# Modulation weights of the mixer's run as fp16 high and low parts, with the conditioning rows as high and low columns of one operand

## The chip, the core and the metric

One core of a Trainium2 chip runs the whole program. TensorE (PE, with its weight loads shown as PEld) multiplies, VectorE (DVE) and ScalarE (ACT) do elementwise work, GpSimd (POOL) does small elementwise work and some DMA issues, SyncE (SP) issues most DMAs in order. The metric is the device time of one execution in microseconds (us); lower is better.

## What is computed

One layer of a hybrid encoder for 512 tokens of a new stream and 8 x 16 tokens of running streams (640 columns, 9 conditioning rows). What matters here:

```python
mod = (jax.nn.silu(c) @ lp['w_ada'] + lp['b_ada'])[:, None, :]
sh_m, sc_m, gt_m, sh_f, sc_f, gt_f = jnp.split(mod, 6, axis=-1)
h = rms_norm(x, lp['g_pre_mix']) * (1 + sc_m) + sh_m
proj = h @ lp['w_in']
...   # attention heads and RWKV-7 heads on proj, both into mix
x = x + gt_m * rms_norm(mix, lp['g_post_mix'])
h = rms_norm(x, lp['g_pre_ffn']) * (1 + sc_f) + sh_f
f, conv_last = conv_ffn(h, conv_prev, lp['w_up'], lp['w_conv_ffn'], lp['w_down'])
x = x + gt_f * rms_norm(f, lp['g_post_ffn'])
```

`w_ada` is 2048 x 12288 in fp32. Its first two of six column blocks (`sh_m`, `sc_m`) are needed before the input projection and are computed in the opening stage; the other four (`gt_m`, `sh_f`, `sc_f`, `gt_f`) are not needed before the output projection has been summed. The change is in these four.

## The kernel before

Large products run on TensorE in fp16 with three passes: a weight tile `[128, 1024]` of fp32 lands in a staging buffer `ws`, ACT writes its high part in fp16 and DVE (`scalar_tensor_tensor`) the low part, both into a buffer `wh`; the matmuls then are high x high, high x low and low x high (`gstep`). `unit` (L379 to L386) does one such tile: a `ws` buffer (`wtile`, 2 buffers, `WS`), a DMA on SP's queue, a `wh` buffer (4, `WH`), the split.

The mixer's run goes from the end of the opening stage to the output projection. Its cover work is 45 chunks of the input projection, each with two units and 96 matmuls in two halves (384 and 256 columns). Between these matmuls stand small jobs: eight RWKV head pairs one after another, each a chain of PE, DVE and ACT steps over blocks of tokens (`S`, `AR`, `VT`, `GB` are its tiles) with round trips through DRAM; eight attention heads; and the generator `ada` (from L1331), the modulation. It works through the four column blocks and for each through 16 row tiles `k`, which makes 64 steps. A step loads two fp32 tiles `wa` of `[128, 1024]` by SP (buffers of their own: tag `wa`, 2) and multiplies `cta` (the conditioning, 128 x 32 columns per `k`, of which 9 are used) with them: four fp32 matmuls of 512 columns, whose outputs stand in four groups of 32 partitions of one PSUM bank. After each four steps DVE adds the bank into `acc`; after 16, four transposes and a DVE addition with the bias finish the block.

The order on PE is fixed in the code. `Interleave` (L143 on) keeps a planned clock: `mm` and the helpers of ACT, DVE and POOL add planned costs to it, and after each k-tile of a projection `pump` lets the waiting generators go on whose planned time has come, `ada` at the lowest priority. A chunk is emitted only when certain heads are far enough (the `while` loop after `ada`); while it may not be, `S.step` moves the planned clock and only the small jobs are emitted. After the 45 chunks come the first products of the output projection (`early`), and then `S.drain(lambda: not S.tasks)` emits what is left of the small jobs before the output projection goes on. The orders on ACT, DVE, POOL and SP are made by a scheduler; each engine runs its list in that order.

## Time and profile before

| | us |
|---|---|
| median of 3 runs (lowest, highest) | 3185.57 (3177.09, 3187.53) |
| the profiled execution | 3185.55 |
| its span, first to last instruction | 3183.7 |
| mixer's run, from the first `wada2` load to the last input-projection matmul | 164 to 1290 |
| first output-projection products and drain of the small jobs | 1290 to 1373 |
| rest of the output projection, FFN | 1373 to 3184 |

The three runs lie within 0.33%. In a timeline row the numbers are start, duration, engine, line, operation, output and inputs, tile size, shape and count; brackets hold idle time before it and what ended it. An fp32 matmul is recorded as two.

### The profile page before, as it was taken

Reading aid. Unit: us, or ns where it says so; the run is one execution under the profiler, and the core shown is the slowest. Engines: PE = TensorE matmul, PEld = TensorE weight load, DVE = VectorE, ACT = ScalarE, POOL = GpSimd, SP = SyncE. Lnnn points to the kernel's source line nnn. Section 1 sums busy time; section 2 is a strip of 40 time slices with the busy share of each in tenths; the row PEclk is TensorE's granted clock in tenths of the full one; section 3 lists DMA queues with packets and bytes.
Section 4 is the critical chain, followed back from the end, with each engine's and each line's share of the span. In section 5 each row is a group of like instructions: output and inputs, shape, how many; then the busy total and the mean of one; then the engine's idle time right before and its main releaser. Section 6 shows DMA issues by size and latency. Waiting matters only on the chain.

```text
span 3183.7 us, 66675 instructions
## 1 busy us (share of the span) xinstructions
PE 3049.7 (96%) x26714; PEld 2075.9 (65%) x26714; DVE 2277.4 (72%) x4347; ACT 1407.5 (44%) x2744; POOL 809.3 (25%) x1508
## 2 busy tenths in 40 slices
PE   6999999999999999789989999999999999999997
PEld 3566666656656566556766677777777777776766
DVE  5454655665556465436788889898999999999875
ACT  4434333343334343334654555454444454544552
POOL 0003213123122120013405424233142231332134
PEclk9999999999999999889999999999999999999998
DMA  9665444534444443355543443533525335254361
GB/s 378 231 207 171 137 142 140 161 127 147 158 141 141 160 135 121 109 175 182 183 149 109 105 130 96 139 107 98 147 93 132 115 92 157 87 124 125 98 229 67
DMA packets 226582, 457.24 MB, mean 144 GB/s; under 512 B 74272, under 2 KB 118432, under 8 KB 226272
## 3 DMA queue, kind: packets, MB, share of 16 engines
q1 hardware_dynamic: 202640, 414.14, 40.4%
q0 software_dynamic: 18160, 32.83, 5.3%
q10 hardware_dynamic: 5472, 6.02, 0.5%
q8 instruction: 209, 3.42, 0.4%
q14 instruction: 101, 0.83, 0.1%
HBM read 425.86 MB, written 26.72 MB: 142 GB/s over the span
## 4 chain that ended last, share of the span: by engine, by line
PE 65%; DVE 9%; DMA 2%; issue 2%; ACT 2%; POOL 1%; SPq 1%; DVEq 0%; ACTq 0%; POOLq 0%
PE ps L269 64%; DVE wh L307 3%; DMA ws<-in_wupT 1%; DVE ws L292 1%; DVE mo L292 1%; PE ps L279 1%; DVE z L307 1%; ACT wh L284 1%; DMA ws<-in_wdnT 1%; SPq L1408 0%; DVE f L307 0%; DVE mo L307 0%; DVE f L292 0%; DMA ckv<-in_ckT 0%; ACT VT L284 0%
## 5 line engine op out<-in xcount | busy, mean ns | idle before, releaser
L269 PEld LDWEIGHTS <-wh 128*128 128x128 f16 x17160 | 1654.5, 98 | 770.7 <-issue 96.6
L269 PE MATMUL ps<-FB,wh 128*128 128x320 f16 x7464 | 1034.4, 301 | 21.7 <-DVE wh L307 5.5
L307 DVE SCALAR_TENSOR_TENSOR wh<-ws,wh 128x1024 f16<-128x1024 f32 (+1 forms) x823 | 803.5, 985 | 219.0 <-ACT wh L284 211.7
L284 ACT ACTIVATE wh<-ws 128x1024 f16<-128x1024 f32 (+1 forms) x823 | 677.8, 834 | 603.6 <-PE ps L269 408.1
L269 PE MATMUL ps<-hT,wh 128*128 128x256 f16 (+3 forms) x4704 | 714.2, 302 | 6.3 <-ACT hT L284 3.9
L269 PE MATMUL ps<-act,wh 128*128 128x320 f16 (+2 forms) x3456 | 475.1, 299 | 6.6 <-ACT wh L284 3.8
L292 DVE TENSOR_TENSOR ws<-ws,ws 128x1024 f32<-128x1024 f32 (+1 forms) x260 | 268.0, 1031 | 13.6 <-DMA ws<-in_wupT 7.8
L269 PE MATMUL ps<-mt,wh 128*128 128x320 f16 x1536 | 219.5, 306 | 13.9 <-DMA mt<-mxd 7.8
L307 DVE SCALAR_TENSOR_TENSOR f<-ps,f 128x320 f32<-128x320 f32 (+2 forms) x336 | 160.7, 483 | 46.9 <-PE ps L269 43.7
L284 ACT ACTIVATE VT<-ps 32x64 f32<-32x64 f32 (+2 forms) x256 | 65.1, 254 | 249.3 <-DVE VT L311 234.1
L307 DVE SCALAR_TENSOR_TENSOR z<-fe,cwv,z 128x656 f32<-128x656 f32 x176 | 162.7, 925 | 4.8 <-ACT z L284 1.6
L420 POOL DMA_DIRECT2D ws<-in_wdnT x96 | 83.3, 867 | 288.1 <-DVE wh L307 131.6
L1456 POOL TENSOR_TENSOR sq<-sq,sq 128x320 f32<-128x320 f32 (+2 forms) x74 | 104.5, 1415 | 194.7 <-ACT sq L284 168.5
L269 PE MATMUL ps<-VT,GB 16*32 16x16 f32 (+4 forms) x2304 | 142.0, 222 | 10.7 <-DVE VT L311 4.0
L284 ACT ACTIVATE act<-z 128x192 f16<-128x192 f32 (+3 forms) x178 | 66.0, 408 | 149.6 <-POOL z L1903 59.0
L269 PEld LDWEIGHTS ps<-VT,GB 32*32 32x32 f32 (+3 forms) x2304 | 80.0, 112 | 78.7 <-issue 39.9
L311 DVE COPY VT<-ps 32x64 f32<-32x64 f32 (+1 forms) x160 | 37.1, 232 | 127.9 <-PE ps L269 119.1
L1920 POOL MEMSET fe<- 128x2 f32 x88 | 12.1, 139 | 443.9 <-DVE z L307 321.5
L296 POOL TENSOR_TENSOR fs<-TU,AU 40x15 f32<-40x15 f32 (+7 forms) x240 | 71.1, 296 | 166.3 <-DMA AU<-gd 149.5
L269 PE MATMUL ps<-wa,cta 128*32 128x256 f32 (+1 forms) x1024 | 111.5, 518 | 0.2 <-DMA wa<-in_wada 0.2
L307 DVE SCALAR_TENSOR_TENSOR S<-S,dcol,ps 128x64 f32<-128x64 f32 x128 | 35.6, 278 | 95.7 <-PE ps L269 94.8
L292 DVE TENSOR_TENSOR act<-z,act 128x320 f16<-128x320 f32 (+3 forms) x160 | 79.2, 524 | 19.8 <-ACT act L284 19.7
(329 smaller groups left out, 3012.0 us busy)
## 6 DMA issues: line engine op xcount, KB each, us to landing
wa<-in_wada SPq DMA_DIRECT2D x192, 512.0 KB
ws<-in_wupT SPq DMA_DIRECT2D x190, 512.0 KB
ws<-in_winT SPq DMA_DIRECT2D x90, 512.0 KB
ws<-in_wdnT SPq DMA_DIRECT2D x96, 384.0 KB
ws<-in_woutT SPq DMA_DIRECT2D x60, 512.0 KB
ws<-in_wdnT POOLq DMA_DIRECT2D x96, 192.0 KB, 3.9
ckv<-in_ckT SPq DMA_DIRECT2D x64, 256.0 KB
ckv<-in_cvN SPq DMA_DIRECT2D x64, 256.0 KB
```

What stands on the lines that cost most here:

```text
L269: nc.tensor.matmul(out, lhsT, rhs, start=start, stop=stop, skip_group_check=True)
L279: nc.tensor.transpose(out, in_, ident)
L284: nc.scalar.activation(out, in_, func, scale=scale, bias=bias)
L292: nc.vector.tensor_tensor(out, a, b, op)
L296: nc.gpsimd.tensor_tensor(out, a, b, op)
L307: nc.vector.scalar_tensor_tensor(out, a, s, b, op0, op1)
L311: nc.vector.tensor_copy(out, a)
L420: nc.gpsimd.dma_start(out, src, accum_op=ADD)
L1456: nc.gpsimd.tensor_tensor(self.acc, self.acc, sq, ADD)
L1920: nc.gpsimd.memset(e[:, 0:2], 0.0)
```

## The change

The fp32 tile of a modulation step now lands in a `ws` buffer (`wtile`, the pool of the input projection's units) and is split by ACT and DVE into fp16 parts in a `wa` buffer of the same bytes (2 buffers). The conditioning is split once into `ct16`: columns 0 to 8 high, 9 to 17 low, the rest zero. A step is then eight fp16 matmuls (high part, then low part, each into the four groups of partitions), and the end of a block adds two column ranges, with 8 small DVE operations in place of one. The planned cost of an fp16 matmul with an output of at most 32 partitions is divided by four.

```diff
         if rhs.dtype == F16:
-            S.pe(n / 2400 + 0.002)
+            S.pe(n / 2400 / (4 if out.shape[0] <= 32 else 1) + 0.002)
...
+    ct16 = mc.tile([P, KD, 32], F16, name="ct16")
...
+        nc.gpsimd.memset(ct16, 0.0)
...
+        act(ct16[:, :, 0:9], cta[:, :, 0:9], AF.Copy)
+        tt(ct16[:, :, 9:18], cta[:, :, 0:9], ct16[:, :, 0:9], SUB)
...
             for k in range(KD):
-                ws = []
+                sts, ws = [], []
                 for u in range(2):
-                    w = lp.tile([P, 1024], F32, tag="wa", bufs=2, name=nm("wa"))
-                    nc.sync.dma_start(w, wada2[i, k, u])
-                    ws.append(w)
+                    sts.append(wtile())
+                    nc.sync.dma_start(sts[u], wada2[i, k, u])
                 S.wait(6.0)
+                for st in sts:
+                    ws.append(lp.tile([P, 2, 1024], F16, tag="wa", bufs=2, name=nm("wa")))
+                    split(ws[-1], st, 1024)
...
-                for u in range(2):
-                    for g in range(2):
-                        q = 2 * u + g
-                        mm(ab[32 * q:32 * q + 32, :], cta[:, k, :], ws[u][:, g * 512:(g + 1) * 512], k % 4 == 0, k % 4 == 3)
+                for z in range(2):
+                    for q in range(4):
+                        g = q % 2
+                        mm(ab[32 * q:32 * q + 32, :], ct16[:, k, :], ws[q // 2][:, z, g * 512:(g + 1) * 512],
+                           k % 4 == 0 and z == 0, k % 4 == 3 and z == 1)
...
-            tt(out.rearrange("p (g s) i -> p g s i", s=4), src, bb.unsqueeze(3).broadcast_to([P, 4, 4, 9]), ADD)
+            o4 = out.rearrange("p (g s) i -> p g s i", s=4)
+            for s in range(4):
+                stt(o4[:, :, s], src[:, :, s, 0:9], 1.0 / SW, bb[:, :, s:s + 1].broadcast_to([P, 4, 9]), MUL, ADD)
+                stt(o4[:, :, s], src[:, :, s, 9:18], 1.0 / SW, o4[:, :, s], MUL, ADD)
```

Three places of the orders, before and after. First SP's loads early in the mixer's run: `in_winT` feeds the input projection, `in_wada2` the modulation. Before:

```order
L383 DMA ws_501_3752<-in_winT 128x1024
L1339 DMA wa_450_3230<-in_wada2 128x1024
L1339 DMA wa_451_3232<-in_wada2 128x1024
L383 DMA ws_503_3757<-in_winT 128x1024
L927 DMA td1_1475<-TU_407_2944 20x16x16 x4
L932 DMA VT_380_2757<-td1_1475 32x10x64 x2
L1339 DMA wa_464_3372<-in_wada2 128x1024
L1339 DMA wa_465_3374<-in_wada2 128x1024
L383 DMA ws_563_4073<-in_winT 128x1024
L383 DMA ws_565_4078<-in_winT 128x1024
```

and after:

```order
L383 DMA ws_746_5114<-in_winT 128x1024
L383 DMA ws_748_5119<-in_winT 128x1024
L1344 DMA ws_775_5310<-in_wada2 128x1024
L1344 DMA ws_776_5312<-in_wada2 128x1024
L383 DMA ws_790_5440<-in_winT 128x1024
L383 DMA ws_792_5445<-in_winT 128x1024
L1344 DMA ws_809_5605<-in_wada2 128x1024
L1344 DMA ws_810_5607<-in_wada2 128x1024
L383 DMA ws_818_5704<-in_winT 128x1024
L383 DMA ws_820_5709<-in_winT 128x1024
L1344 DMA ws_836_5871<-in_wada2 128x1024
L1344 DMA ws_837_5873<-in_wada2 128x1024
```

Before, the modulation's loads went to `wa` and stood at any place among the others; after, both kinds go to the two `ws` buffers, in turn by pairs.

Second PE, at the end of the first long stretch without projection matmuls (it lies behind the twelfth of the 45 chunks in both orders). `wh` is a unit of the chunk that follows, `ident` marks a transpose. Before:

```order
L269 MATMUL ps_714_4962<-ckv_666_4679,aTs_708_4923 32x128 x4
L269 MATMUL ps_714_4962<-ckv_667_4682,aTs_708_4923 32x128 x4
L269 MATMUL ps_714_4962<-ckv_668_4685,aTs_708_4923 32x128 x4
L269 MATMUL ps_714_4962<-ckv_669_4688,aTs_708_4923 32x128 x4
L269 MATMUL ps_714_4962<-vtk_506_3766,aTs_708_4923 32x128 x4
L269 MATMUL ps_694_4857<-S_711_4948,AR_512_3794 64x64 x2
L269 MATMUL ps_694_4857<-VT_514_3796,GB_513_3795 32x64 x2
L269 LDWEIGHTS wh_731_5039
L269 MATMUL ps_734_5047<-hT_92,wh_731_5039 128x384
```

and after:

```order
L269 MATMUL ps_665_4712<-wa_682_4777,ct16_99 32x512
L269 MATMUL ps_738_5057<-GB_559_4085,VT_560_4086 32x96 x10
L269 MATMUL ps_739_5058<-GB_559_4085,VT_560_4086 32x96 x10
L269 MATMUL ps_740_5083<-S_631_4557,AR_558_4084 64x64 x2
L269 MATMUL ps_740_5083<-VT_560_4086,GB_559_4085 32x64 x2
L279 MATMUL ps_741_5095<-ident_69,osbs_514_3799 128x128 x2
L269 LDWEIGHTS wh_747_5116
L269 MATMUL ps_750_5124<-hT_92,wh_747_5116 128x384
```

The last work ahead of the chunk was attention and one RWKV step; now it is the eight fp16 matmuls of a modulation step, a few RWKV rows and a transpose.

Third PE at the end of the drain, where the output projection (`mt`) goes on. Before:

```order
L269 MATMUL ps_2535_16786<-ckv_2521_16735,aTs_2534_16782 32x128 x4
L269 MATMUL ps_2535_16786<-ckv_2522_16738,aTs_2534_16782 32x128 x4
L269 MATMUL ps_2535_16786<-ckv_2523_16741,aTs_2534_16782 32x128 x4
L269 MATMUL ps_2535_16786<-ckv_2524_16744,aTs_2534_16782 32x128 x4
L269 MATMUL ps_2535_16786<-vtk_2434_16253,aTs_2534_16782 32x128 x4
L279 MATMUL ps_2543_16831<-ident_69,osbs_2448_16373 128x128 x2
L269 LDWEIGHTS wh_2436_16285
L269 MATMUL ps_2443_16303<-mt_16254,wh_2436_16285 128x320
```

and after:

```order
L269 LDWEIGHTS ct16_99
L269 MATMUL ps_2634_17327<-wa_2671_17484,ct16_99 32x512
L279 MATMUL ps_2672_17496<-ident_69,acc_2142_14499 128x128 x4
L269 LDWEIGHTS wh_2534_16801
L269 MATMUL ps_2541_16819<-mt_16770,wh_2534_16801 128x320
```

Before, the last small job was attention's transpose of `osbs`; now two whole modulation steps and the transposes of `acc` stand behind it. Before, the 64th modulation step stood almost six chunks ahead of the last one; now eight steps stand behind the last chunk: one before the first products of the output projection, two among them, five in the drain. From the FFN's first matmul on PE's order is the same.

## Rows read from the trace of the kernel before

**Rows 1.** Spans and mean granted TensorE clock of the cores.

```profile
core 0: 3183.7 us, clock 0.978
```

**Rows 2.** Stretches: us, busy us (instructions) of PE, PEld, DVE, ACT, POOL; clock; DMA share; GB/s.

```profile
164.00:1290.00 1126.00, 1104.02 (x12250) 709.69 (x12248) 642.53 (x1763) 436.68 (x1088) 242.11 (x700) 0.98 0.47 149
1290.00:1373.00 83.00, 52.67 (x392) 34.81 (x391) 29.76 (x103) 20.14 (x60) 0.81 (x2) 0.75 0.38 112
1700.00:3183.00 1483.00, 1451.58 (x10640) 1042.02 (x10637) 1300.77 (x1902) 714.45 (x1203) 466.88 (x694) 0.99 0.42 117
```

**Rows 3.** Groups by shape, 164 to 1290 us: busy us, mean ns | idle before.

```profile
L269 PE MATMUL ps<-hT,wh 128*128 128x384 f16 x2111 | 389.0, 330 | 0.0
...
L307 DVE SCALAR_TENSOR_TENSOR wh<-ws,wh 128x1024 f16<-128x1024 f32 x86 | 105.4, 1225 | 55.1 <-ACT wh L284 54.5
L284 ACT ACTIVATE wh<-ws 128x1024 f16<-128x1024 f32 x87 | 91.8, 1055 | 45.6 <-PE ps L269 44.3 <-ACT ytk L284 0.9
L269 PE MATMUL ps<-wa,cta 128*32 128x512 f32 x512 | 72.7, 638 | 0.0
```

**Rows 4.** Timeline, one modulation step and the projection matmuls behind it.

```profile
608.23 0.16 PEld L269 LDWEIGHTS ps<-wa,cta 128*32 128x32 f32 x8
608.24 1.07 PE L269 MATMUL ps<-wa,cta 128*32 128x512 f32 x8
...
609.23 0.66 PE L269 MATMUL ps<-hT,wh 128*128 128x384 f16 x3
```

**Rows 5.** Timeline, an unbroken run of fp16 matmuls and what follows.

```profile
1329.66 6.29 PE L269 MATMUL ps<-mt,wh 128*128 128x320 f16 x45
1335.78 0.39 PE L269 MATMUL ps<-vtk,aTp 128*128 128x128 f32 x2
```

**Rows 6.** Waits of SP's queue, 150 to 1165 us: total us, times, longest.

```profile
SPq L1339 <- PE ps L269: 226.9, 62, 15.3
SPq L383 <- DVE wh L307: 170.9, 42, 12.5
```

**Rows 7.** Who waited for `ws`, 150 to 1165 us: us, times.

```profile
  PEld ps L269: 3.9, 6
...
  PE ps L269: 2.5, 1
```

**Rows 8.** DMA issues, 164 to 1290 us: count, KB each, median us to landing.

```profile
mxd<-hl POOLq DMA_DIRECT2D x7, 320.0 KB, 4.4
...
out_wkvs<-sn POOLq DMA_DIRECT2D x8, 256.0 KB, 2.4
```

**Rows 9.** Stretches without projection matmuls, columns as in rows 2.

```profile
411.00:424.80 13.80, 9.88 (x103) 5.36 (x104) 7.27 (x15) 7.50 (x15) 2.50 (x6) 0.75 0.53 177
645.70:663.50 17.80, 14.15 (x202) 9.35 (x201) 13.39 (x45) 12.00 (x33) 8.74 (x29) 0.90 0.67 234
890.20:899.00 8.80, 8.80 (x195) 6.83 (x194) 6.27 (x16) 4.92 (x9) 7.15 (x22) 1.00 0.36 121
...
1337.70:1372.70 35.00, 19.08 (x150) 12.25 (x149) 14.78 (x57) 10.45 (x33) 0.11 (x1) 0.65 0.21 64
```

**Rows 10.** Timeline, one RWKV step and the start of the next.

```profile
604.07 0.33 PE L269 MATMUL ps<-S,AR 64*64 64x64 f32 x4
...
606.02 0.56 PE L269 MATMUL ps<-VT,GB 64*64 64x64 f32 x8
...
607.74 0.33 PE L269 MATMUL ps<-S,AR 64*64 64x64 f32 x4
```

**Rows 11.** Waits of the engines, 165 to 1165 us: total us, times, longest.

```profile
DVE wh L307 <- ACT wh L284: 49.0, 30, 10.0
```

**Rows 12.** Timeline, a wait of PE in the first stretch of rows 9.

```profile
414.56 0.29 PE L269 MATMUL ps<-VT,GB 64*64 64x64 f32 x2 [2.50 <-ACT wh L284]
```

**Rows 13.** Timeline, the end of the drain.

```profile
1371.23 0.69 PE L279 MATMUL ps<-ident,osbs 128*128 128x128 f32 x2 [3.69 <-DVE osbs L292]
1372.72 39.56 PE L269 MATMUL ps<-mt,wh 128*128 128x320 f16 x267 [0.80 <-ACT mt L284]
```

More of the change, by code (lines that the diff above doesn't have):

```diff
@@ L1361, in ada @@
                 tpe(tp[:, s * P:(s + 1) * P], acc[:, s * P:(s + 1) * P])
-            src = tp.rearrange("p (s g i) -> p g s i", s=4, g=4)[:, :, :, 0:9]
+            src = tp.rearrange("p (s g i) -> p g s i", s=4, g=4)
             bb = vec[:, V_BADA + 16 * (i + 2):V_BADA + 16 * (i + 3)].rearrange("p (g s) -> p g s", s=4)
-            tt(out.rearrange("p (g s) i -> p g s i", s=4), src, bb.unsqueeze(3).broadcast_to([P, 4, 4, 9]), ADD)
+            o4 = out.rearrange("p (g s) i -> p g s i", s=4)
+            for s in range(4):
+                stt(o4[:, :, s], src[:, :, s, 0:9], 1.0 / SW, bb[:, :, s:s + 1].broadcast_to([P, 4, 9]), MUL, ADD)
+                stt(o4[:, :, s], src[:, :, s, 9:18], 1.0 / SW, o4[:, :, s], MUL, ADD)
             if kind == "sh":
```

## The prediction, made before the changed kernel ran

> **What bounds the kernel now.** I read the spans first: one core, 3183.7 us, mean clock 0.978 of full speed [rows 1]. The profiled execution took 3185.55 us, so 1.9 us lie around the span, and the median of the runs is the same within 0.02 us. The sum below is made against 3185.55. Then the stretches [rows 2]. In the mixer's run, where the modulation is, PE is busy 1104.0 of 1126 us; DVE has 642.5 us and ACT 436.7 us, 57% and 39%. So PE sets the time there, and its idle time is only 22 us. In the drain PE is busy 52.7 of 83 us at a clock of 0.75: there chains of small steps set the time. Behind 1700 us PE is busy 98%, and since its order is the same from the FFN's first matmul on, I leave that part as it is. Next I looked at why PE waits so little. The waits on the staging buffers show that weights are early: in 1015 us PE and its loads waited some 6 us for what comes from `ws` [rows 7]. The loads of the projection's weights are issued when DVE has emptied a `ws` buffer, those of the modulation when PE has read a `wa` buffer [rows 6]: two queues of buffers that do not hold up one another's data, though SP issues in one order.
>
> **The PE work of a step.** Before, the eight records of a step start at 608.24 and the projection goes on at 609.23: 1.00 us of PE [rows 4]. A step is four fp32 matmuls of 512 columns, so four of them run side by side. After, it is eight fp16 matmuls of 512 columns. In an unbroken run 45 fp16 matmuls of 320 columns take 6.12 us from start to start [rows 5], 0.425 ns a column, 0.218 us for 512. If four run side by side as the fp32 ones do, a step takes 2 x 0.218 = 0.44 us; one after another, 8 x 0.218 = 1.74 us. No fp16 matmul of the kernel before has a 32-column tile, so this is a bound from both sides: 64 steps save 64 x 0.56 = 36 us or cost 64 x 0.74 = 47 us. I take 0.50 us, near the nearest row (the same tile shape in fp32), which gives **-32 us**. All of it lies on PE's path in the mixer's run.
>
> The step's eight weight loads were done in 0.16 us, beside the first matmuls [rows 4]. The Trainium skill (TensorE: Matmul & The Clock Gate, Part 3, "The mechanism") says that weight loads overlap matmuls in flight only when their row groups differ, and here all have the same rows; by that the matmuls of a step would stand one after another, and the term would be the +47 us. The row speaks against it for fp32.
>
> **What ACT and DVE get.** 128 tiles are split: on ACT 1.06 us and on DVE 1.23 us each [rows 3], 135 and 157 us, which raises DVE to about 800 of 1126 us. Neither becomes the bound as a sum, and the cover is PE's own work. But both run in order, and a chain step that PE waits for can stand behind a split. That is seen once clearly now: PE waited 2.50 us for ACT, which was in a `wh` split [rows 12]; and DVE stood 49.0 us at `wh` splits whose high part ACT had not written [rows 11]. With 128 splits more than the 86 there are, the first scales to 2.5 x 128 / 86 = 4 us, the second, if PE felt all of it, to 73 us. I take **+5 us**, since almost all of the 49 us left no mark on PE. The one-time split of the conditioning, the added memset and the eight small DVE operations at each block's end stand beside projection matmuls and cost nothing; in the last block they are in the drain, but PE does not wait for them.
>
> **The stretches without cover.** PE's order is the place where most moves. At a few places no projection matmul stands in it, since the next chunk may not be emitted yet; there PE runs small jobs and waits for other engines. Before, three such stretches in the mixer's run have 15 waiting rows or more (18, 19, 17) and the drain has 30; in time they are 13.8, 17.8, 8.8 and 35.0 us [rows 9]. Busy time multiplied by the granted clock gives the work at full speed: 7.4, 12.7, 8.8 and 12.4 us. So 6.4, 5.1, 0 and 22.6 us were lost there, idle or at the lower of the two clock levels, 34 us in all: 0.36, 0.27 and 0 us a waiting row in the mixer's run, 0.75 in the drain. The changed order has six such stretches with 24, 30, 23, 27, 34 and 26 waiting rows, 164 together, and 43 in the drain. The reason is in the steps: a modulation step now passes through staging, ACT and DVE before PE can run it, the planner lays it out longer (counted in columns of the projection, steps stand some 10 us apart on average instead of 7.6), and the RWKV chain falls behind the chunks. 18 RWKV steps lie in those six stretches against 6 in the three before; one step takes 3.67 us from start to start [rows 10], most of it other engines' time. At 0.36 us a row, that of the stretch with most RWKV steps, the six lose 59 us; at 0.75 the drain loses 32 us; less the 34 us of now, **+57 us**. The bounds: at the mean of the three stretches, 11.5 / 54 = 0.21 us, and a drain as now, 34 + 23 - 34 = +23; at 0.75 for all, 155 - 34 = +121. In the drain two modulation steps stand behind attention's last transpose, where PE now goes on after 1.5 us [rows 13]; that is inside the 43 rows.
>
> **The weights behind the modulation.** In SP's order the loads of projection and modulation now alternate by pairs in the two `ws` buffers. A chunk's first load therefore waits until the modulation's pair before it has been split; that split needs the two `wa` buffers, which the modulation step before it on PE still reads. So from that step on PE's order the chunk's first weights need two splits in a row (1.06 + 1.23 = 2.3 us), a load of 512 KB, and again 2.3 us. For the load the nearest rows are 2.4 us for 256 KB and 4.4 us for 320 KB [rows 8]; I take 4.4 us as an estimate (ends 3 and 6), together 9.0 us. The Trainium skill (DMA: Bandwidth & Descriptors, "Anatomy of one DMA") gives 2.0 us and bytes / 436e9, though for GpSimd's path, so 3.2 us; by that the need would be 7.8 us, and the rows do not tell them apart. Mostly a chunk has 10 to 15 us of PE's work as lead. But at seven places, the first chunk after each of the six stretches or the like, and the first products of the output projection, the order leaves less than 3 us of PE's own work between that step and the chunk; the second place of the orders above is one, with 32 RWKV records and a transpose, some 2.5 us, and as much in waits for ACT and DVE. 9.0 - 5.0 = 4 us of each is exposed, **+28 us**, nothing if the waits counted above cover it, 7 x 9 = 63 us if none does. Before, the same loads had been issued a chunk ahead.
>
> **Sum.** -32 + 5 + 57 + 28 = +58 us on 3185.55: **3244 us**.
>
> **Rivals.** *PE keeps its cover.* If the stretches lose no more than now (the jobs in them are work PE has to do anyway, and what stands there no longer interrupts the projection elsewhere) and the weights come in time, only the -32 us stays: 3153 us. For it speaks that the mixer's run has just 22 us of idle time now; against it, that this rests on weights a chunk ahead, and the order takes that away. *Gains and losses cancel.* With the low ends of the stretches (+23) and half of the four us of each place (+14), -32 + 5 + 23 + 14 = +10, about 3190 us; it decides at some 0.2 us a waiting row. *The fp16 tiles don't run side by side.* Then the term of PE is +47 in place of -32: 3323 us; it is also what the skill's rule named above would make of it. It decides from 1.00 us a step, and the change would not do what it is built on. The fp32 records speak against it.
>
> **How the numbers follow.** A measurement of this kernel can tell about 0.3%, 9.6 us, from no change. Chances: the forecast, 3200 to 3310, 0.64; the tiles one after another 0.07; gains and losses cancel, 3176 to 3195, 0.12; PE keeps its cover 0.17. That gives slower 0.72 (with a part of the cancelling cases just past the bound put to the middle), same 0.11, faster 0.17. The range reaches down to 3170, where the PE-bound case is cut off, and up to 3315: the forecast's upper terms without the one-after-another case.
>
> **What would show it.** Right: eight records of a step in about 0.5 us; six stretches of 20 to 35 us without projection matmuls in the mixer's run, with a clock well below 0.98 in them; PE waiting for `wh` or for loads into `ws` at the first chunk behind each; SP's waits for `wh` and `wa` splits on DVE in the place of those for PE; the drain longer by some 10 us. Wrong: the mixer's run ends about 30 us earlier with PE still busy 98% (then leads and waiting rows were no measure), or a step takes over 1 us.

## The result, and the profile after

The changed kernel took 3310.57 us, median of 4 runs (3304.33 to 3313.12), against 3183.86 us of the kernel before: 1.0395 times as long, 95% interval 1.0381 to 1.041. That is 127 us more. The forecast was 3244, 58 us more: the sign was right and the time lay in the range, 4 us below its upper end, but the excess is over twice the forecast's.

Nearly all of it arises ahead of the FFN. By stretches, in the columns of [rows 2]:

```profile
164.00:1290.00 1126.00, 1020.93 (x11088) 672.31 (x11086) 700.72 (x1708) 496.41 (x1076) 257.08 (x675) 0.92 0.41 126
1373.00:1500.00 127.00, 85.01 (x705) 53.36 (x702) 70.82 (x199) 52.00 (x120) 2.45 (x6) 0.75 0.52 165
1700.00:3183.00 1483.00, 1452.54 (x10674) 1040.68 (x10673) 1330.97 (x1963) 729.89 (x1233) 433.64 (x665) 0.99 0.42 118
```

In the first line PE is busy 1020.9 of 1126 us, against 1104.0 in [rows 2], and the granted clock is 0.92 in place of 0.98. The drain now ends at 1495.2 us, before at 1372.7; from there to the end it is 1813 us, before 1811. Behind 1700 us the two profiles read alike.

The step itself does what the change says. Timeline of a step on PE (start, duration, operation):

```profile
250.68 0.61 PE L269 MATMUL ps<-wa,ct 128*32 128x512 f16 x8
251.22 0.50 PE L269 MATMUL ps<-hT,wh 128*128 128x256 f16 x3
```

The projection goes on 0.54 us after the step's start, where it was 1.00 us in [rows 4]. By the rate of [rows 5] eight such matmuls one after another are 1.74 us, so over three run at a time, as the four groups of partitions side by side would.

The splits, from the page's groups (busy us, mean ns | idle time before them):

```profile
L307 DVE SCALAR_TENSOR_TENSOR wa<-ws,wa 128x1024 f16<-128x1024 f32 x128 | 156.2, 1236 | 57.7 <-ACT wa L284 57.1
L284 ACT ACTIVATE wa<-ws 128x1024 f16<-128x1024 f32 x128 | 128.7, 1048 | 116.1 <-PE ps L269 92.1
```

Their durations are those of the forecast (157 and 135 us). New is the idle time: ACT stands 92 us at splits whose `wa` buffer PE has not read yet. Of ACT's waits from 165 to 1500 us a second is new as well, at the projection's own splits, where ACT had stood 107.1 us for PE before (us in total, times, longest):

```profile
ACT wh L284 <- DMA ws<-in_winT: 105.4, 63, 8.4
```

PE in turn waits 18.6 us for `wh` from 164 to 1500 us, each time at a projection matmul:

```profile
PE ps L269 <- ACT wh L284: 15.4, 5, 8.2
PE ps L269 <- DVE wh L307: 3.2, 7, 0.8
```

12.6 of them stand at the first projection matmul behind a stretch listed below (447.9, 716.6, 879.2 and 1047.4 us). Before, no projection matmul waited so; the 2.50 us of [rows 12] are a chain step's.

And the stretches without projection matmuls, six in the mixer's run and the drain, in the columns of [rows 9], which had three and the drain:

```profile
407.90:447.90 40.00, 21.86 (x327) 16.46 (x325) 31.83 (x93) 22.68 (x58) 13.97 (x46) 0.67 0.38 111
673.30:716.60 43.30, 24.81 (x323) 17.86 (x323) 30.38 (x98) 20.15 (x53) 18.84 (x52) 0.63 0.29 81
859.00:879.20 20.20, 14.67 (x270) 11.58 (x271) 17.22 (x56) 15.74 (x39) 12.19 (x26) 0.83 0.40 129
1018.00:1047.40 29.40, 20.79 (x270) 15.81 (x268) 20.99 (x60) 19.95 (x51) 16.34 (x40) 0.75 0.44 132
1260.10:1305.90 45.80, 31.23 (x400) 22.99 (x400) 34.97 (x101) 27.65 (x70) 14.32 (x48) 0.66 0.40 110
1381.10:1413.10 32.00, 14.25 (x161) 9.93 (x162) 17.22 (x56) 14.13 (x39) 1.35 (x3) 0.71 0.79 239
1446.30:1495.20 48.90, 26.68 (x215) 15.40 (x214) 28.06 (x72) 20.09 (x46) 0.11 (x1) 0.67 0.44 143
```

Span less busy time times clock gives 25.4, 27.7, 8.0, 13.8, 25.2, 21.9 and 31.0 us, 153 us lost in all, where the forecast took 91. It is tempting to stop here and say that the stretches were priced too low. The experiments say otherwise.

### The profile page after: what moved, and what is told of

Read it like the earlier page. It is cut to its first block, busy times and chain, and to the rows that moved or that the text cites. A ratio compares the mean times of both kernels' runs of the same rounds, so it can differ in the third digit from the quotient of the medians.

```text
span 3308.0 us, 67117 instructions
## 1 busy us (share of the span) xinstructions
PE 3070.2 (93%) x26714; PEld 2104.5 (64%) x26714; DVE 2427.1 (73%) x4504; ACT 1536.6 (46%) x2873; POOL 840.8 (25%) x1509
## 4 chain that ended last, share of the span: by engine, by line
PE 69%; DVE 13%; DMA 7%; ACT 4%; issue 3%; POOL 3%; SPq 0%; ACTq 0%; DVEq 0%; POOLq 0%
PE ps L269 68%; DVE wh L307 3%; DMA ws<-in_winT 3%; ACT wh L284 1%; DVE wa L307 1%; DVE ws L292 1%; POOL fs L296 1%; PE ps L279 1%; DVE z L307 1%; DMA ws<-in_wupT 1%; POOL TU L296 1%; DVE mo L292 1%; ACT wa L284 1%; DMA ws<-in_woutT 1%; DMA ws<-in_wada 1%
## 5 line engine op out<-in xcount | busy, mean ns | idle before, releaser
L269 PE MATMUL ps<-FB,wh 128*128 128x320 f16 x7464 | 1032.2, 301 | 23.9 <-DVE FB L292 5.5
L269 PE MATMUL ps<-hT,wh 128*128 128x256 f16 (+3 forms) x4704 | 726.4, 306 | 20.5 <-ACT wh L284 13.9
L307 DVE SCALAR_TENSOR_TENSOR wa<-ws,wa 128x1024 f16<-128x1024 f32 x128 | 156.2, 1236 | 57.7 <-ACT wa L284 57.1
L284 ACT ACTIVATE wa<-ws 128x1024 f16<-128x1024 f32 x128 | 128.7, 1048 | 116.1 <-PE ps L269 92.1
L269 PE MATMUL ps<-VT,GB 16*32 16x16 f32 (+4 forms) x2304 | 149.7, 228 | 30.8 <-ACT VT L284 11.5
L475 POOL COPY sho<-ext 128x1 f32<-128x1 f32 x26 | 10.8, 417 | 509.5 <-ACT ext L284 509.5
L296 POOL TENSOR_TENSOR fs<-TU,AU 40x15 f32<-40x15 f32 (+7 forms) x240 | 87.8, 366 | 116.0 <-DMA AU<-gd 99.5
```

The lines of the kernel that those rows point to most:

```text
L269: nc.tensor.matmul(out, lhsT, rhs, start=start, stop=stop, skip_group_check=True)
L284: nc.scalar.activation(out, in_, func, scale=scale, bias=bias)
L296: nc.gpsimd.tensor_tensor(out, a, b, op)
L307: nc.vector.scalar_tensor_tensor(out, a, s, b, op0, op1)
L475: nc.gpsimd.tensor_copy(sho[:, idx, 0:1], e[:, TP:TP + 1])
```

## The experiments

The theories: **T1**, the planned order (the planner books the splits, and the chains fall behind); **T2**, the `ws` ring that projection and modulation now share; **T3**, the splits stand ahead of the RWKV and attention chains' steps on ACT's and DVE's in-order queues; later **T4**, a form of T3: not the splits' work, but the queues standing at tiles that are not there yet. "Order of before" means that all of TensorE's instructions but the modulation's own stand as in the kernel before, "order of after" the same for the changed kernel.

| run | order | splits | steps | us | ratio to before, interval |
|---|---|---|---|---|---|
| changed kernel | after | real, shared ring | fp16 | 3310.6 | 1.0395 (1.0381 to 1.041) |
| x1_order_before | before | real, shared ring | fp16 | 3284.9 | 1.0319 (1.0304 to 1.0334) |
| x2_own_staging | after | real, own buffer | fp16 | 3293.6 | 1.0341 (1.0325 to 1.0357) |
| x3_both | before | real, own buffer | fp16 | 3269.1 | 1.0269 (1.0254 to 1.0284) |
| x7_plan_only | after | none | fp32 | 3229.9 | 1.0148 (1.0131 to 1.0165) |
| x4_fp16_only | before | none | fp16 | 3174.2 | 0.9968 (0.9956 to 0.9981) |
| x5_splits_beside | before | beside | fp32 | 3275.6 | 1.0281 (1.0262 to 1.0299) |
| x21_planned_beside | after | beside | fp32 | 3321.4 | 1.0437 (1.0404 to 1.0471) |
| x14_wait_only | before | beside, 8 columns | fp32 | 3212.3 | 1.0098 (1.008 to 1.0116) |
| x19_act_long | before | beside, DVE 8 columns | fp32 | 3233.9 | 1.0163 (1.014 to 1.0187) |
| x20_dve_long | before | beside, ACT 8 columns | fp32 | 3266.9 | 1.0266 (1.0242 to 1.0289) |

"Beside" are splits of the fp32 tiles into a scratch that nothing reads. Six more runs stand at the end of this section. The excess in us given below is over the median of the kernel before that was measured beside each run, 3183 to 3184 us. In the cuts of code, `...` marks lines left out; `rsplit` is a split's two instructions without a booking.

### Order and ring taken out of the changed kernel

x1 lets the planner see the old step: the same two instructions of a split are issued without a booking, and the step is booked at its old price.

```diff
...
-                    split(ws[-1], st, 1024)
+                    rsplit(ws[-1], st, 1024)
...
-                        mm(ab[32 * q:32 * q + 32, :], ct16[:, k, :], ws[q // 2][:, z, g * 512:(g + 1) * 512],
-                           k % 4 == 0 and z == 0, k % 4 == 3 and z == 1)
+                        nc.tensor.matmul(ab[32 * q:32 * q + 32, :], ct16[:, k, :], ws[q // 2][:, z, g * 512:(g + 1) * 512],
+                                         start=k % 4 == 0 and z == 0, stop=k % 4 == 3 and z == 1, skip_group_check=True)
+                        if z == 0:
+                            S.pe(512 * 4 / 2400 / 4 + 0.005)
```

> The changed kernel, but the planner is not told of the change: it books a modulation step at the old price and without the splits, so that TensorE's other instructions stand in exactly the order of the kernel before. Splits, shared ring and fp16 steps are all there. Theory T1 (the planned order does it: booked split time pushes the RWKV and attention chains behind whole rows of modulation and makes the stretches without projection matmuls longer): most of the excess goes, 3195 to 3235 us. Theory T2 (the ring shared with the projections' weights) and theory T3 (the splits stand ahead of the chain's steps on ACT's and DVE's in-order queues): the order is not the cause, 3275 us or more.

x2 gives the modulation's tiles a buffer of their own; it is one, and `cta` moves to another pool to make room for it.

```diff
...
-                    sts.append(wtile())
+                    sts.append(lp.tile([P, 1024], F32, tag="wst", bufs=1, name=nm("wst")))
```

> The changed kernel in its own order, with one change: the modulation's fp32 tiles land in a buffer of their own (one, where the shared ring has several) and no longer in the ring of the projections' weights. T2 (ring): the 105 us that ACT waited for ring tiles shrink to a few tens and 40 to 90 us come back, 3220 to 3270 us. T1 and T3: less than 15 us come back, 3295 to 3315 us; a single buffer could even cost a little, since both tiles of a step load one after the other.

x3 has both edits.

> Both edits: order of the kernel before, fp32 tiles in a buffer of their own; the fp16 steps and the splits stay. T1 and T2 together leave only the gain of the fp16 steps (about 30 us) and the splits' contention: 3155 to 3195 us. T3 (splits ahead of the chain's steps on the in-order queues): the splits are all there still, so 3230 us or more.

Measured: 3284.9, 3293.6 and 3269.1 us. The old order brings back 26 us, the own buffer 17, both 41, and 86 us of excess stay when both causes are gone. T1 fails in x1, T2 in x2; T3 alone has the right side in all three (x2 just under its 3295). What the own buffer can say on the ring is limited, since with one buffer the tiles load one after another: in x3 ACT stood 174.2 us at them. In x2 PE waits only 1.0 us for `wh` from 164 to 1500 us, in place of 18.6, but it waits for the modulation's own tiles, 19.2 us in place of 2.7:

```profile
PE ps L269 <- ACT wa L284: 14.0, 5, 5.4
PE ps L269 <- DVE wa L307: 5.2, 4, 3.1
```

So the ring does hold up the projection's weights, and the 17 us are what is left after the own buffer's waits.

### The order alone

x7 keeps the changed kernel's bookings and issues the old instructions.

```diff
...
-                    ws.append(lp.tile([P, 2, 1024], F16, tag="wa", bufs=2, name=nm("wa")))
-                    split(ws[-1], st, 1024)
+                for u in range(2):
+                    S.op("A", 1024 * 0.838e-3 + 0.09)
+                    S.cur.t += 0.13
+                    S.op("V", 1024 * 1.04e-3 + 0.07)
```

> The kernel before in the order of the changed kernel: the planner books the splits and the fp16 steps, but the instructions are the old ones (fp32 tiles in their own two buffers, fp32 steps, no split). TensorE's other instructions stand in exactly the order of the changed kernel. T1 (planned order): 3245 to 3290 us, most of the excess without a single split. T2 and T3: within 20 us of the kernel before, 3165 to 3205 us.

Measured: 3229.9 us, 47 us more than before, under T1's lower end of 3245 and well above what T2 and T3 had. The same seven stretches in this run:

```profile
398.30:432.40 34.10, 23.07 (x328) 17.14 (x328) 27.75 (x93) 17.91 (x52) 11.69 (x38) 0.75 0.36 106
640.60:673.70 33.10, 22.69 (x325) 15.33 (x325) 23.39 (x88) 14.79 (x46) 11.96 (x44) 0.81 0.39 110
812.60:831.00 18.40, 14.60 (x271) 11.25 (x271) 15.41 (x57) 14.01 (x37) 9.33 (x26) 0.94 0.60 191
964.50:987.60 23.10, 17.02 (x270) 11.85 (x268) 17.16 (x53) 16.06 (x46) 13.43 (x36) 0.96 0.58 193
1193.90:1235.20 41.30, 33.34 (x399) 23.25 (x399) 27.87 (x94) 20.84 (x63) 16.22 (x50) 0.66 0.43 129
1309.00:1326.60 17.60, 12.46 (x161) 8.52 (x161) 11.05 (x47) 10.39 (x34) 1.20 (x3) 1.00 0.98 310
1364.10:1413.60 49.50, 31.17 (x217) 15.38 (x215) 17.81 (x62) 12.03 (x38) 0.11 (x1) 0.78 0.52 177
```

Span less busy time times clock: 16.8, 14.7, 4.7, 6.8, 19.3, 5.1 and 25.2 us, 93 us. The forecast had 91 for them. So the stretches by themselves were priced right, the six short by 8 us and the drain long by 7. The other 60 us that they lose in the changed kernel come with what x7 lacks: splits, ring and short steps. x21 below takes them apart.

### The fp16 steps alone

```diff
...
-                    sts.append(wtile())
-                    nc.sync.dma_start(sts[u], wada2[i, k, u])
-                S.wait(6.0)
-                for st in sts:
                     ws.append(lp.tile([P, 2, 1024], F16, tag="wa", bufs=2, name=nm("wa")))
-                    split(ws[-1], st, 1024)
+                    nc.sync.dma_start(ws[u].bitcast(F32).rearrange("p z n -> p (z n)"), wada2[i, k, u])
+                S.wait(6.0)
...
-                        mm(ab[32 * q:32 * q + 32, :], ct16[:, k, :], ws[q // 2][:, z, g * 512:(g + 1) * 512],
-                           k % 4 == 0 and z == 0, k % 4 == 3 and z == 1)
+                        nc.tensor.matmul(ab[32 * q:32 * q + 32, :], ct16[:, k, :], ws[q // 2].rearrange("p z (n t) -> p (z n) t", t=2)[:, g * 512:(g + 1) * 512, 1],
+                                         start=k % 4 == 0 and z == 0, stop=k % 4 == 3 and z == 1, skip_group_check=True)
...
```

> The order of the kernel before, fp32 tiles loaded into their own two buffers as before, no split at all: the eight fp16 matmuls of a step read the upper halves of the fp32 words in place. Left out: the split, so the modulation is computed from other weights. Against the kernel before only the step's work on TensorE differs. If a step costs 0.5 us in place of 1.0 and the rest keeps its time: 3150 to 3160 us. If the fp32 steps had covered waits that now come to the light, less comes back: 3165 to 3190 us.

Measured: 3174.2 us, 9.5 us less than before (6 to 14 by the interval). 59 of the 64 steps have the short records (0.63 us for the eight), and from a step's start to the matmul behind it are 0.57 us in the median, where it was 1.00. So some 28 us of work are gone from PE, but the median shows only a third of it. The profiled execution was the fastest of six, its span 21.5 us under that of before. Up to the last projection matmul, at 1268.8 us in x4 and 1290.1 before, PE is busy

```profile
164.00:1268.80 1104.80, 1074.84 (x12245) 710.08 (x12243) 643.54 (x1789) 435.72 (x1085) 242.77 (x700) 0.98 0.47 151
```

29 us less and idle 8 us more (30 for 22). Why the median shows 9.5 us only, the runs do not settle.

### Splits beside the old kernel

x5 is the kernel before, and behind the loads of a step:

```diff
...
                 S.wait(6.0)
+                for w in ws:
+                    rsplit(lp.tile([P, 1, 1024], F16, tag="scr", bufs=1, name=nm("scr")).broadcast_to([P, 2, 1024]), w, 1024)
```

> The kernel before with its fp32 steps and its order; each modulation tile is also split by ACT and DVE into one scratch buffer that nothing reads (the low part in place over the high part). TensorE does not wait for these splits, so what they cost is ACT's and DVE's time ahead of the RWKV and attention chains, and the wait of those in-order queues for the tile's load and for one another. Theory T3 (splits ahead of the chain's steps): 3240 to 3300 us, since order and ring together gave back only 41 of 127 us. Against it (the cost is TensorE's own wait for split tiles): 3185 to 3210 us.

Measured: 3275.6 us, 92 us more, with no instruction of TensorE changed and none waiting for a split. This is T3's number. x3, with real splits in the old order, agrees: it is 95 us over x4, which has its short steps, two `wa` buffers for the loads and no split. What x5 has and the changed kernel has not is the one scratch, at which ACT waited 27.0 us for DVE (164 to 1150 us). How it happens is seen at the first large loss. Timeline of ACT in the kernel before:

```profile
272.83 2.45 ACT L284 ACTIVATE VT<-ps 32x128 f32<-32x128 f32 x8 [1.31 <-PE ps L279]
...
276.97 0.49 ACT L284 ACTIVATE vT<-ps 128x384 f32<-128x384 f32 x1
```

of ACT in x5:

```profile
281.11 1.06 ACT L369 ACTIVATE scr<-wa 128x1024 f16<-128x1024 f32 x1 [11.00 <-DMA wa<-in_wada]
282.19 2.45 ACT L284 ACTIVATE VT<-ps 32x128 f32<-32x128 f32 x8
...
286.33 0.49 ACT L284 ACTIVATE vT<-ps 128x384 f32<-128x384 f32 x1
```

and of PE in x5:

```profile
278.77 0.83 PE L269 MATMUL ps<-hT,wh 128*128 128x256 f16 x6
286.87 1.12 PE L269 MATMUL ps<-hT,wh 128*128 128x384 f16 x3 [7.27 <-ACT vT L284]
287.92 1.94 PE L269 MATMUL ps<-wa,cta 128*32 128x512 f32 x8
```

In the kernel before, the RWKV chain's `VT` copies start at 272.8 us and `vT`, the copy of a projection chunk's output out of PSUM, at 277.0. In x5 a split stands ahead of them on ACT, and its tile lands at 281.1: ACT waits 11.00 us at the head of its queue, the copies run 9.4 us late, and PE, whose order is fixed, stands 7.27 us until `vT` has emptied the bank that its next matmul writes. The modulation step that reads the tile comes on PE only at 287.9. The tile was late since its load stood in SP's queue. The step before had left both `wa` buffers by 267.1, but ahead of the load SP waited for the RWKV chain on GpSimd and then 3.6 us for that chain's round trip; the load was issued at 277.3 and landed 3.8 us later:

```profile
SPq L931 <- POOL TU L296: 8.0, 1, 8.0
277.33 0.93 SPq L1343 DMA_DIRECT2D wa<-in_wada  x2
```

Before, the same load was issued at 275.8, and nothing on ACT waited for it. That is the place of this one loss; over the RWKV part, 164 to 1060 us, SP stood 193.2 us at these loads for PE's matmuls (53 times) and 52.7 us for the split on DVE (16). Either way ACT had been working ahead of PE, and the split ties it to a load that comes late for ACT and in time for PE.

Over the RWKV part it adds up (columns of [rows 2], the kernel before first, then x5):

```profile
164.00:1060.00 896.00, 874.90 (x9727) 558.02 (x9725) 513.43 (x1390) 345.96 (x856) 210.25 (x609) 0.98 0.48 153
```

```profile
164.00:1060.00 896.00, 832.29 (x8766) 521.82 (x8764) 581.45 (x1349) 415.02 (x857) 216.29 (x529) 0.93 0.43 138
```

PE's idle time grows from 21 to 64 us, and the clock falls from 0.98 to 0.93. In the same stretch PE waited for chain steps on ACT and DVE; of its waits, before (first line) and in x5:

```profile
PE ps L269 <- ACT VT L284: 3.9, 7, 0.8
```

```profile
PE ps L269 <- ACT VT L284: 13.4, 14, 2.7
PE ps L269 <- DVE VT L311: 12.0, 10, 3.4
PE ps L269 <- DVE UT L307: 9.2, 4, 6.2
```

For DMAs it waited 2.0 us in all, before 1.4, so late loads reach PE by way of the two engines, not by themselves. By busy time times clock, x5 has done 857 - 774 = 83 us less work by 1060 us: 43 of it is idle time, 40 the lower clock. The same matmul that before starts at 260 us starts 1 us earlier in x5, that of 664 us 58 us later, that of 1060 us 90 us later, that of 1500 us 97 us later, counted in matmuls on both timelines. So the RWKV part loses all along, and the 12 of 128 splits that stand behind the matmul of 1060 us go with the last 7 us.

### Waiting or work

x14 has the same splits at the same places on 8 columns, so waits for the tiles stay and most of the work goes: an operation of 8 columns takes 0.21 us on ACT and 0.17 us on DVE, 26 and 23 us for 128.

```diff
...
+                    h8 = lp.tile([P, 8], F16, tag="scr", bufs=1, name=nm("scr"))
+                    nc.scalar.activation(h8, w[:, 0:8], AF.Copy, scale=SW, bias=0.0)
+                    nc.vector.scalar_tensor_tensor(h8, w[:, 0:8], SW, h8, MUL, SUB)
```

> The counterpart: the kernel before plus splits of the first 8 columns of each modulation tile, into a scratch, at the same place. The waits for the loads and between ACT and DVE are those of a full split, the work is next to nothing. T4 (queues standing at tiles that are not there yet): 3235 to 3275 us. T3, plain: 3185 to 3205 us. If both halves matter, the two runs together should make about the 92 us.

Measured: 3212.3 us, 29 us. It is between the theories: the waits, with these small operations, make a third of the 92 us, with ACT standing longer at the tiles than in x5. ACT's waits from 164 to 1150 us, x5 and then x14:

```profile
ACT scr L369 <- DMA wa<-in_wada: 117.6, 45, 11.0
```

```profile
ACT scr L1344 <- DMA wa<-in_wada: 173.4, 87, 8.9
```

The other 63 us are the work, or work and waits together. x19 and x20 give the full 1024 columns to one engine:

```diff
...
+                for w in ws:
+                    nc.scalar.activation(scr[:, 0:8], w[:, 0:8], AF.Copy, scale=SW, bias=0.0)
+                    nc.vector.scalar_tensor_tensor(scr[:, 0:1024], w[:, 0:1024], SW, scr[:, 0:1024], MUL, SUB)
```

(x20; x19 has the two numbers exchanged. Both use one scratch for all the splits.)

> The kernel before with splits beside it into a scratch, same order on TensorE, same places and waits; ACT's operation has its full 1024 columns, DVE's only 8. If the 63 us of work are DVE's (it is the busier engine, 57 against 39%): 3212 to 3225 us, as with 8 columns on both. If they are ACT's: 3255 to 3275 us. If each engine's work counts by its time: 3230 to 3250 us.

> The other half: 8 columns on ACT, the full 1024 on DVE, same places and waits. If the work is DVE's: 3255 to 3275 us; if ACT's: 3212 to 3225 us; if each counts by its time: 3230 to 3255 us, and the two runs' excess over 3212 adds up to about 63 us.

Measured: 51 and 84 us, so 21 and 54 us over the 29 of x14. x19 lies in its range for work that counts by its time, x20 in its range for DVE's work. DVE's work counts most, though DVE is busy only 588.6 of 896 us there. A part of it may come by way of the scratch, where ACT waited 31.6 us for DVE in x20 and 6.5 in x19; no run parts that. The two add up to 75, not 63: they overlap a little.

### Whether booking helps

x21 is x7 plus the splits beside it: the planner books them, and they are there.

```diff
...
+                for w in ws:
+                    h = lp.tile([P, 1024], F16, tag="scr", bufs=1, name=nm("scr"))
+                    nc.scalar.activation(h, w, AF.Copy, scale=SW, bias=0.0)
+                    nc.vector.scalar_tensor_tensor(h, w, SW, h, MUL, SUB)
```

> Splits beside the old kernel's fp32 steps, in the order of the changed kernel, whose planner books them; own tiles, no shared ring. The order alone gave 3230 us. If booked splits are free at the places that the plan made for them: 3225 to 3245 us. If order and splits add up as in the old order: 47 + 92, 3310 to 3330 us. From the changed kernel itself (3311 us, less 10 to 21 us that the fp16 steps give, less some 17 us of the shared ring): 3300 to 3315 us.

Measured: 3321.4 us, 138 us more. 47 for the order and 92 for the splits would be 139. Booking the splits cost 47 us and saved none of the 92. The same seven stretches:

```profile
413.10:452.70 39.60, 22.86 (x327) 16.92 (x326) 32.55 (x97) 21.82 (x56) 12.18 (x38) 0.70 0.40 114
674.90:716.50 41.60, 24.87 (x325) 16.49 (x325) 28.50 (x97) 18.60 (x51) 13.44 (x47) 0.71 0.32 88
863.10:885.80 22.70, 16.63 (x272) 12.73 (x272) 18.34 (x65) 14.98 (x39) 10.17 (x28) 0.86 0.52 161
1025.60:1054.30 28.70, 22.62 (x269) 15.94 (x268) 20.99 (x60) 18.69 (x49) 15.88 (x38) 0.75 0.51 164
1272.20:1315.20 43.00, 29.35 (x400) 20.99 (x400) 32.16 (x97) 24.61 (x66) 18.63 (x53) 0.74 0.38 118
1395.80:1417.00 21.20, 15.44 (x161) 10.66 (x161) 13.31 (x49) 12.39 (x36) 1.07 (x3) 0.80 1.00 306
1457.30:1512.60 55.30, 33.12 (x215) 16.36 (x214) 28.83 (x72) 22.02 (x48) 0.11 (x1) 0.71 0.46 156
```

They lose 23.6, 23.9, 8.4, 11.7, 21.3, 8.8 and 31.8 us, 130 us. So the splits add 37 us inside the stretches and the rest of their 92 outside; the last 23 of the changed kernel's 153 come with the ring and the short steps, 12.6 of them being PE's waits for `wh` at the stretches' ends.

### Runs that missed their aim, and tries at a better kernel

**x8** let x3's splits read numbers that lie in the chip.

```diff
...
+        src = vec[:, None, 0:128].broadcast_to([P, 8, 128])
+        nc.scalar.activation(hl[:, 0].rearrange("p (a b) -> p a b", a=8), src, AF.Copy, scale=SW / 1024, bias=0.0)
```

> The kernel with the order of before and one own staging buffer, but the splits read numbers that lie in the chip all the time; the modulation's loads still run into the staging buffer, and nobody reads them. Left out: the modulation's weights. No split waits for a load any more, all else is there. If what is left of the excess (86 us) is ACT standing at splits whose load is late (174 us of waits in that kernel): 3175 to 3210 us. If it is the splits themselves in the queues: 3240 to 3270 us.

Measured: 3290.2 us, 21 us above x3. It changed more than was meant: with nothing to hold them the modulation's loads ran ahead, and other loads were late (ACT's waits):

```profile
ACT lora L284 <- DMA lw<-in_lora: 68.2, 8, 23.1
```

In x3 that wait was 20.6 us. The run tells nothing on the splits.

**x13** put the work of the splits in, without waits:

```diff
...
+                    nc.scalar.activation(sa.rearrange("p (a b) -> p a b", a=8), vec[:, None, 0:128].broadcast_to([P, 8, 128]), AF.Copy, scale=0.0625, bias=0.0)
+                    nc.vector.scalar_tensor_tensor(sd.rearrange("p (a b) -> p a b", a=5), vec[:, None, 0:128].broadcast_to([P, 5, 128]), 0.0625, sd.rearrange("p (a b) -> p a b", a=5), MUL, SUB)
...
```

> The kernel before, with the same order on TensorE, plus the work of the splits without their waits: at the place of each split ACT scales 1024 columns and DVE works on 640 and 384 columns, from numbers that lie in the chip, each engine into a scratch of its own. No load, no other engine and no TensorE is waited for. If the work itself holds up the chain (T3, plain): most of the 92 us that splits beside the old kernel cost, 3240 to 3275 us. If it is the waits of ACT's and DVE's queues at the splits (T4): 3185 to 3220 us.

Measured: 3241.0 us, 58 us. But the places are others. Operations that wait for nothing were put earlier in each engine's order when the program was built; 53 of the 128 stand on ACT between 220 and 300 us, where x5 has 10 splits:

```profile
220.00:300.00 80.00, 67.25 (x638) 44.31 (x636) 77.53 (x173) 77.20 (x125) 22.84 (x47) 0.89 0.38 123
460.00:640.00 180.00, 167.71 (x1842) 105.08 (x1839) 105.94 (x258) 64.46 (x141) 36.16 (x94) 0.95 0.41 130
```

ACT is busy 77.2 of the first stretch's 80 us, and in the later stretch no more than in the kernel before. The agreement of 58 + 29 with 92 is no proof; x14 against x5 is the comparison that counts.

**x9** was to move x5's splits to the step's own place.

```diff
...
                 else:
                     yield 0
+                for w in ws:
+                    rsplit(lp.tile([P, 1, 1024], F16, tag="scr", bufs=1, name=nm("scr")).broadcast_to([P, 2, 1024]), w, 1024)
```

> The kernel before plus the splits that nothing reads, as in the run that added 92 us, with the same order on TensorE and the same work on ACT and DVE. Only the place of a pair of splits in ACT's and DVE's order is another: directly ahead of the modulation step that reads the tiles, and no longer directly behind the issue of their loads, some 6 us of the plan earlier, where ACT stood 118 us for loads. Theory T4 (a split that stands in the queue before its tile is there holds up every chain step behind it): most of the 92 us go, 3185 to 3215 us. Theory T3 in its plain form (the 2.3 us of a split's work themselves hold up the chain): 3250 to 3280 us.

Measured: 3270.7 us. In ACT's order all but two of the 128 splits stand at the place they have in x5, so this is x5 once more (ACT stood 111.7 us at the tiles), and no test of T4. The excess of 87 us repeats that of x5.

**x10** and **x12** rework the changed kernel with one own buffer: a split, the next tile's load, a pause, the next split; x10 without bookings, x12 with them and with shorter pauses.

```diff
...
                 for u in range(2):
+                    if u:
+                        S.wait(4.0)
+                        yield 0
                     ws.append(lp.tile([P, 2, 1024], F16, tag="wa", bufs=2, name=nm("wa")))
-                    split(ws[-1], st, 1024)
+                    rsplit(ws[-1], st[0], 1024)
+                    load()
+                S.wait(2.5)
...
```

> The changed kernel with the modulation's tiles in a staging buffer of their own, and each split emitted only when its tile should be there: split, then the next tile's load, then the plan goes on with other work before the next split. The planner books the splits at nothing, and a fp16 step at the old price; the order on TensorE is near that of the kernel before, not equal to it. T4: ACT no longer stands at splits, so little is left beside the gain of the fp16 steps (10 to 21 us in the run that did those alone): 3170 to 3205 us. T3 in its plain form: 3250 us or more.

> As the run before, but the planner books the splits and the fp16 steps at their prices, so that the order on TensorE is near that of the changed kernel. T4 with the cost that the planned order alone showed (47 us): 3205 to 3250 us. If truthful bookings help once the splits stand at their planned place: below the run before, 3165 to 3200 us. T3 in its plain form: 3260 us or more.

Measured: 3274.1 and 3362.9 us (ratios 1.0279 and 1.0557). ACT still stood 160.5 us at the tiles in x10. With bookings it was worse again, though the pauses differ too.

**x15** moves the splits beside the old kernel to GpSimd.

```diff
...
+                    nc.gpsimd.tensor_copy(hs, w)
+                    nc.gpsimd.tensor_tensor(hs, w, hs, SUB)
```

> The kernel before, same order on TensorE, with the full splits beside it on GpSimd in place of ACT and DVE (a copy to fp16 and a subtraction, into a scratch that nothing reads). GpSimd has the least to do there (210 of 896 us), but its work per column is more, and some steps of the attention and RWKV chains run on it too. If it is the place in ACT's and DVE's queues that costs: 3185 to 3215 us. If any in-order engine of the chain that has to stand at the late tiles costs as much: 3250 us or more.

Measured: 3436.0 us, ratio 1.08. Waits of GpSimd and then of PE, 164 to 1150 us:

```profile
POOL scr L1344 <- DMA wa<-in_wada: 236.4, 50, 17.8
```

```profile
PE ps L269 <- DMA VT<-td: 100.2, 13, 20.5
```

A step of the RWKV chain goes by way of GpSimd to `td` and back into `VT`; with splits ahead of it PE waits 100 us where it waited 0.3. The engine with the most idle time was the worst place.

No run with the splits in it beats the kernel before. Whether tiles loaded a whole step ahead, into two staging buffers beside the two `wa` buffers, would save the waiting third was not tried.

## Why the prediction was wrong

**What bounds the kernel** held: PE's fixed order in the mixer's run, nothing behind it. Of the 6 us of [rows 7], 2.5 are the chain step's wait of [rows 12] and no wait for weights, which makes the weights earlier still.

**The PE work, -32.** Mechanism right, 0.54 us a step for the 0.50 taken, so some 29 us of work. As time it measured -10 in x4. The rule of the Trainium skill that was weighed there (TensorE: Matmul & The Clock Gate, Part 3, "The mechanism"), read as the prediction reads it, would have had the tiles one after another; the records of 0.61 us for eight speak against that reading for fp16 as well.

**What ACT and DVE get, +5.** This is the step that failed. The mechanism, a chain step that stands behind a split, is named there; its size was wrong. It measured +92 in the old order (x5) and 138 - 47 = 91 in the new one (x21). Some 29 of it is standing at late tiles, which the forecast did not count at all, and 63 work. The forecast had a number that would have warned, 49.0 us of DVE's waits in [rows 11] scaled to 73, and set it aside because those waits "left no mark on PE". That 73 is near 92 is luck: it is another wait, DVE's for ACT at projection splits. The new splits stand in front of steps and copies that PE's order expects just in time, as seen at 281 us in x5, and idle share of an engine was no cover for that. The 2.50 us of [rows 12] were scaled by the count of splits alone, as if there were one such place. By x21 against x7, 37 of the 92 us lie inside the coverless stretches and the rest outside them, in what the forecast had taken as covered.

**The stretches without cover, +57.** The order alone cost 47 us as a whole (x7), and its stretches lost 93 us against 91 forecast. This step was right, at 0.41 us a waiting row in the six for the 0.36 taken, and with less than taken in the drain. With the splits a row costs 0.60 (x21), in the changed kernel 0.74.

**The weights behind the modulation, +28.** The mechanism is there, and at places that were named: ACT stood 105.4 us at loads of `ws`, before at most 2.0, and PE 18.6 us at `wh`, two thirds of it at the first chunk behind four of the six stretches. The load that was taken at 4.4 us took 3.8 in the one place read in x5. But an own buffer brings back 16 to 17 us only, since it has waits of its own. The sum of what was measured apart, -10 + 92 + 47 = +129, leaves nothing for the ring beside 127; with 17 it is 146. So what the ring is worth stays open, 0 to 17 by these sums, and the parts do not add exactly; the fp16 steps' worth has the same doubt (x3 is 6 us under x5, x2 is 28 under x21).

**The rivals.** PE did not keep its cover, gains and losses did not cancel, and the tiles did not run one after another. The time of this third rival, 3323, is close to the measured one by accident.

## What to carry to other kernels

An engine that is 39 or 57% busy need not have free time if it runs in order and serves a chain whose consumer has a fixed order. Here a split of 1.06 us on ACT and 1.23 us on DVE cost 0.72 us of the whole (92 us for 128), 0.04 in the forecast. Count every place where a chain step stands behind the added operation, and check first whether its input will be there when the engine reaches it, which can be ahead of where the consumer is: in x5 ACT reached the tile 18 us before PE's step. Before precision is bought off TensorE with splits on other engines, put the splits beside the old kernel, reading nothing back: that one run gave three quarters of the answer here. A planner that is told of the extra work does not make room for it for nothing; here the kernels in which it was told were 25 to 47 us slower than the like ones in which it was not, in four pairs, and x12 was 89 us slower than x10, which it is less like.

## What the runs showed of the hardware

The waits were paid nearly twice. In x5, 43 us more idle time of PE came with some 40 us lost to the clock (0.93 for 0.98 over 832 us of busy time): from 278 to 290 us, with PE idle 7.45 of 12 us, the granted clock was 0.63 on the mean, between its two levels (1.2 and 2.4 GHz), and it was 0.76 over the next 10 us, in which PE was busy 9.3. Of the records of a whole step in the changed kernel, five took 1.04 to 1.08 us in place of 0.61; one more, 3.47 us long, has a wait inside.

GpSimd needed 1.04 us for the fp16 copy of 1024 columns and 2.13 us for the subtraction (medians in x15), against 1.06 us on ACT and 1.22 us on DVE for the two halves of a split.
